# A quadrant swap of an 8192 x 8192 array: the right halves move to GpSimd's queue in eight-row copies

## The chip, the core and the metric

The kernel runs on one core of one Trainium2 chip. A core has five engines with an instruction queue each (TensorE, VectorE, ScalarE, GpSimd and SyncE) and 16 DMA engines that move data. The metric is the device time of one execution in microseconds. Three executions of the kernel before took 814.30, 814.51 and 814.64 us; their median is 814.51 us.

## The reference

```python
x = np.random.randn(8192, 8192).astype(np.float32)

def reference(x):
    return np.fft.ifftshift(x)
```

For even sizes this shifts both axes by half: `out[r, c] = x[(r + 4096) % 8192, (c + 4096) % 8192]`. Nothing is computed. The four quadrants of 64 MB each change places across the diagonal, so 268.44 MB are read and 268.44 MB are written.

## The kernel before

Input and output both lie in device memory, with 8192 float32 values, or 32 KB, to a row. The kernel uses no on-chip buffer: every transfer goes from the input straight to the output. Half a row is 16 KB, and since the column shift is exactly half a row, the left half of an output row is the right half of one input row, and the other way round.

The helper `copy` (line 26) takes a queue, a first output row, a first output column (0 for a left half, `hc` = 4096 for a right half) and an access pattern. It works out where the source begins (line 28) and issues one DMA on that queue (line 29). The pattern `back` (line 34) has three dimensions: 16 neighbouring rows, then 16 steps backwards by 16 rows each, then the 16 KB of a half row. So one copy moves the halves of 256 rows, 4 MB, and it is written as 16 shares of 16 rows each: share e takes the rows that lie e above the base row, then e - 16, e - 32 and so on down.

The outer loop (line 36) walks the output from the bottom to the top in stretches of 1024 rows, which are four blocks of 256. The inner loop (line 37) takes the four blocks in the order 3, 2, 1, 0. For each it issues the left half of block n on SyncE's queue (line 38) and the right half of block (n + 2) % 4 on ScalarE's queue (line 39). That makes 32 copies on each queue. No copy depends on another. The framework counts the landing of copies on semaphores, of which these copies use eight in turn, and a queue waits before it issues a copy until the earlier copy on the same semaphore has landed.

In the profile's lines the letter q after an engine's name (SPq, ACTq, POOLq) means the engine's instruction queue. q1 and q10 are the DMA queues on which the packets of the two issuing engines run. A packet is one half row of 16 KB, or a few bytes that count a landing.

Of the kernel before, what the change touches and what calls it, by code (L numbers as in the profile page):

```python
# [1 line left out]

# [4 lines left out]


ENGINES = 16


@with_exitstack
def kernel(
    ctx: ExitStack,
    tc: tile.TileContext,
    x: bass.AP,
    out: bass.AP,
):
    nc = tc.nc
    R, C = x.shape  # L20
    hr = R // 2
    hc = C // 2
    per = 16
    rows = ENGINES * per

    def copy(queue, row, col, dims):

        src = (row + hr) % R * C + (col + hc) % C
        queue.dma_start(
            out=bass.AP(out.tensor, out.offset + row * C + col, dims),  # L30
            in_=bass.AP(x.tensor, x.offset + src, dims),
        )

    back = [[C, ENGINES], [-ENGINES * C, per], [1, hc]]

    for first in range(R - 4 * rows, -1, -4 * rows):
        for n in (3, 2, 1, 0):
            copy(nc.sync, first + n * rows + rows - ENGINES, 0, back)
            copy(nc.scalar, first + (n + 2) % 4 * rows + rows - ENGINES, hc, back)


# [1 line left out]
_INS = ['x']  # L43
_OUTS = [((8192, 8192), 'float32')]


def kernel(**inputs):
    import numpy as _np
    import concourse.bacc as _bacc
    import concourse.tile as _tile  # L50
    from concourse import mybir as _mybir
    from concourse.bass_utils import run_bass_kernel_spmd as _run

    nc = _bacc.Bacc("TRN2", target_bir_lowering=False, num_devices=1)  # L54
    arrays, args = {}, []
    for name in _INS:
        a = _np.ascontiguousarray(inputs[name])
        if a.dtype.kind in "iu":
            a = a.astype(_np.int64)
        arrays[f"in_{name}_dram"] = a  # L60
        args.append(nc.dram_tensor(f"in_{name}_dram", a.shape, _mybir.dt.from_np(a.dtype), kind="ExternalInput").ap())
    for i, (shape, dtype) in enumerate(_OUTS):
        dt = _mybir.dt.from_np(_np.dtype(dtype))
        args.append(nc.dram_tensor(f"out_{i}_dram", shape, dt, kind="ExternalOutput").ap())
    with _tile.TileContext(nc) as tc:
        kernel(tc, *args)
    r = _run(nc, [arrays], core_ids=[0])
    got = tuple(r.results[0][f"out_{i}_dram"] for i in range(len(_OUTS)))
    return got[0]
```

## Time and profile before

| What | Value |
|---|---|
| median of three executions | 814.51 us |
| the profiled execution | 813.9 us |
| its span, first to last instruction | 812.1 us |
| bytes read, bytes written | 268.44 MB, 268.44 MB |
| mean rate of the copies | 331 GB/s |
| memory traffic over the span, both directions | 661 GB/s |
| DMA packets | 17408, of which 16384 are half rows |
| copies issued by SyncE, by ScalarE | 32, 32 |
| one issue on SyncE, on ScalarE (median) | 571 ns, 578 ns |
| issue to landing of one copy (median) | 101.0 us |

The span leaves out 1.8 us of the profiled execution's 813.9 us, which lie before the first and after the last instruction. The profiled execution lies 0.6 us under the median. The page's DMA row gives the mean busy share of the 16 DMA engines in 40 equal slices of the span, in tenths, and the row under it what they moved in each slice in GB/s. A copied byte counts once there, though it is both read and written. Busy shares are worked out from packet records, so over a short stretch they can come out above 1.

### The profile page before, as it was taken

How to read it: one execution, taken by the hardware profiler on the slowest of the kernel's cores; microseconds unless marked ns; L12 is line 12 of the kernel's file. 1: busy time of each engine (PE TensorE's matmuls, PEld its weight loads, DVE VectorE, ACT ScalarE, POOL GpSimd, SP SyncE). 2: the span in 40 equal slices, each digit the busy share in tenths (PEclk: the TensorE clock that was granted, in tenths of full speed). 3: DMA queues.
4: the chain of work that ended last, by engine and by line, in shares of the span. 5: the costliest groups of instructions: out<-in, count | busy, mean ns of one | idle time of the engine just before them, and what ended most of it. 6: DMA issues, size and time to landing. Idle time of an engine off the chain costs nothing. (4 is left out here: it accounts for less than half of the span.)

```text
span 812.1 us, 109 instructions
## 1 busy us (share of the span) xinstructions
POOL 0.2 (0%) x4
## 2 busy tenths in 40 slices
POOL 0000000000000000000000000000000000000000
DMA  9999999999999999999999999999999999999998
GB/s 306 332 329 337 333 332 335 328 324 337 329 336 337 332 334 334 334 336 331 332 329 330 337 328 334 339 331 333 332 320 333 330 331 330 336 332 337 334 333 286
DMA packets 17408, 268.44 MB, mean 331 GB/s; under 512 B 1024, under 2 KB 1024, under 8 KB 1024
## 3 DMA queue, kind: packets, MB, share of 16 engines
q1 hardware_dynamic: 8704, 134.22, 49.9%
q10 hardware_dynamic: 8704, 134.22, 49.1%
HBM read 268.44 MB, written 268.44 MB: 661 GB/s over the span
## 5 line engine op out<-in xcount | busy, mean ns | idle before, releaser
L54 POOL MEMSET const-bfloat16-1.0<- 128x1 bf16 x1 | 0.1, 102 | 0.0
L54 POOL MEMSET const-uint8-127<- 128x1 uint8 x1 | 0.1, 102 | 0.0
L54 POOL MEMSET const-float32-1.0<- 128x1 f32 x1 | 0.1, 99 | 0.0
L54 POOL MEMSET const-float32-0.0<- 128x1 f32 x1 | 0.1, 98 | 0.2 <-issue 0.2
## 6 DMA issues: line engine op xcount, KB each, us to landing
out_dram<-in_x_dram ACTq DMA_DIRECT2D x32, 4096.0 KB, 101.0
out_dram<-in_x_dram SPq DMA_DIRECT2D x32, 4096.0 KB, 101.0
```

The source lines that it names most:

```text
L54: nc = _bacc.Bacc("TRN2", target_bir_lowering=False, num_devices=1)
```

## The change

```diff
-    back = [[C, ENGINES], [-ENGINES * C, per], [1, hc]]
+    half = ENGINES // 2
     for first in range(R - 4 * rows, -1, -4 * rows):
         for n in (3, 2, 1, 0):
-            copy(nc.sync, first + n * rows + rows - ENGINES, 0, back)
-            copy(nc.scalar, first + (n + 2) % 4 * rows + rows - ENGINES, hc, back)
+            copy(nc.sync, first + n * rows + rows - ENGINES, 0, [[C, ENGINES], [-ENGINES * C, per], [1, hc]])
+            right = first + (n + 2) % 4 * rows + rows - half
+            for part in (0, half):
+                copy(nc.gpsimd, right - part, hc, [[C, half], [-ENGINES * C, per], [1, hc]])
```

The left halves are copied by the same 32 copies of 4 MB, on the same queue, in the same order. The right halves leave ScalarE's queue for GpSimd's. Each copy of 256 right halves becomes two of 128. The outermost dimension of their pattern has 8 rows in place of 16, and the steps stay at 16 rows. Part 0 takes the upper eight rows (the higher row numbers) of every 16 and part 8 the lower eight. That makes 64 copies of 2 MB, written as eight shares each; by the description of the change they go to the two groups of eight DMA engines in turn. The order of the blocks is the same. ScalarE then issues nothing.

## The prediction

> **What bounds the kernel now.** I read the page first: no engine computes, so the DMA rows carry everything. These are its lines of the span, the DMA slices, the queues and the memory traffic.
>
> ```profile
> span 812.1 us, 109 instructions
> DMA  9999999999999999999999999999999999999998
> GB/s 306 332 329 337 333 332 335 328 324 337 329 336 337 332 334 334 334 336 331 332 329 330 337 328 334 339 331 333 332 320 333 330 331 330 336 332 337 334 333 286
> DMA packets 17408, 268.44 MB, mean 331 GB/s; under 512 B 1024, under 2 KB 1024, under 8 KB 1024
> q1 hardware_dynamic: 8704, 134.22, 49.9%
> q10 hardware_dynamic: 8704, 134.22, 49.1%
> HBM read 268.44 MB, written 268.44 MB: 661 GB/s over the span
> ```
>
> The reader is to see that the DMA engines are busy from end to end (9 tenths or more in 39 of 40 slices; the queues' shares sum to 99.0%), and that the two queues split this evenly. A half row of 16384 bytes thus takes 0.990 x 812.1 x 16 / 16384 = 0.785 us of one DMA engine. The trace's packet records say what that consists of: the shortest half row took 0.608 us (26.9 GB/s), a third of them at most 0.612 us, the median one 0.726 us. So an engine can go 29% faster than it does on average. What holds it back is shared by the 16; I read it as the memory at 661 GB/s, though no row names it.
>
> Next the stretches in time (length, busy engines, clock, DMA share, GB/s), for the ends:
>
> ```profile
> 1.00:2.00 1.00, 0.00 (x0) 1.00 0.00 0
> 2.00:3.00 1.00, 0.00 (x0) 1.00 0.87 262
> ...
> 806.00:808.00 2.00, 0.00 (x0) 1.00 1.04 369
> 808.00:809.00 1.00, 0.00 (x0) 1.00 0.75 197
> 809.00:810.00 1.00, 0.00 (x0) 1.00 0.31 131
> 810.00:811.00 1.00, 0.00 (x0) 1.00 0.04 16
> 811.00:812.10 1.10, 0.00 (x0) 1.00 0.00 0
> ```
>
> Some 2 us pass before the first bytes, about 2 us at the end are lost to engines that finish unevenly, and 1.1 us follow the last bytes. All the rest is rate. The 38 inner slices have a mean of 332.4 GB/s, a lower quartile of 330.25, and ends of 320 and 339.
>
> Last the issues (nanoseconds, minimum, median and maximum), and what SyncE's queue waits for (total us, times, longest):
>
> ```profile
> L29 ACTq DMA_DIRECT2D out_dram<-in_x_dram x32: 577/578/884, 0.7 to 713.4; - x32
> L29 SPq DMA_DIRECT2D out_dram<-in_x_dram x32: 571/571/666, 0.7 to 709.0; - x32
> DMA to landing us min/median/max: 25.4/101.0/103.2
> SPq L29 <- DMA out_dram<-in_x_dram: 689.7, 28, 25.2
> ```
>
> SyncE issues for 32 x 0.571 = 18 us in all and waits 690 us for earlier copies: after its first four copies, each of the other 28 waits. The landing time agrees with eight copies in flight: 8 x 4.194 MB at 332 GB/s take 101 us. Issue is far from the bound; there is always a queue of work ahead of each DMA engine.
>
> **The change part by part.** The sum starts at the profiled execution's 813.9 us, 0.6 under the median; I add 0.6 at the end.
>
> *ScalarE's 32 issues go.* They took 32 x 0.578 = 18.5 us on an engine that does nothing else. Hidden; gain 0.
>
> *GpSimd gets 64 issues.* No row shows an issue on GpSimd. The nearest rows are POOL's memset at 0.10 us and ScalarE's longest issue at 0.884 us: 64 of them are 6 to 57 us, spread over 800. One 2 MB copy is needed every 12.6 us (2.097 MB at half of 332 GB/s), so the copies in flight hide them: cost 0. Without that cover it would be up to 57 us. Only the first issue can be seen. If GpSimd's first bytes come 0 to 1 us after SyncE's, the DMA engines already have left halves, and half of the delay returns at the end when right halves run alone: 0 to 0.5, I take 0.3.
>
> *More landing counts.* A copy of before counts with 16 small packets (1024 for 64). After, there are 96 copies: 512 packets for the left and 64 x 8 or 64 x 16 for the right, so 0 to 512 more. One takes 9 ns in the packet records: 512 x 9 / 16 engines = 0.3 us at most. I take 0.3.
>
> *SyncE's waits.* If SyncE has the eight semaphores alone, it waits for the copy eight before, not four, and 33.6 MB of left halves are in flight. Behind the waiting issue only further left copies are queued, and 8 copies of cover stand ahead. Cost 0. The same holds for GpSimd if it may keep several copies in flight: behind its waiting issue are only further right copies, and ScalarE waits for nobody. With less than one copy for each group, the cover is gone (last rival).
>
> *A packet of GpSimd's queue against one of ScalarE's.* No row shows it. The nearest is the difference of the two hardware queues, 49.9% against 49.1% for the same packets: 0.8% of 812.1 us, 6.5 us in time, or 13 ns for each of the 512 half rows that a queue has per engine. I take 0, since the engines wait for something shared, and keep -6.5 and +6.5 for the range.
>
> *Which rows are under way together.* In the diff this is the real change for the memory. Before, DMA engine e takes left and right halves of rows that are e modulo 16, in turn; 16 engines always stand on 16 different remainders. After, if the first group takes part 0, engine e has left halves of rows e but right halves of rows e + 8 modulo 16. When one engine has a left half and the engine eight further a right half, both stand on rows whose distance is a multiple of 16, or of 512 KB; this can happen about half of the time. The bounds are the slices: all at the best, 339 GB/s, is -1.9% or -16 us; all at the worst, 320, is +3.9% or +31 us. Nothing excludes either sign. The lower quartile is 0.65% under the mean, 5.2 us; I take half of it, since the meetings need opposite halves: +2.6. The row it is nearest to is the mean, as the bytes, packet sizes and number of streams per engine stay.
>
> The Trainium skill speaks against the change here. "DMA: Bandwidth & Descriptors", section "Latency and other measured facts", says that copies whose parallel streams lie a large power of two apart lose rate, 207 against 214 GB/s at a distance of 512 KiB and half at 4 MiB, and calls channel aliasing an inference. Carried over in full, 3.4% would make the sum about 842 us, an estimate. This trace shows no run with and without such meetings; its own slices bound the effect instead.
>
> *The end.* GpSimd's queue has drains of 34 to 66 ns now; with copies to wait for it may take as ScalarE's, up to 0.4 us. I take 0.3.
>
> Sum: 813.9 + 0.3 + 0.3 + 2.6 + 0.3 = 817.4, and 0.6 to the median: 818.0 us, 0.4% slower.
>
> **The rivals.** *A. Nothing of it matters.* All DMA engines stay busy at the same mean rate, and only the small terms remain: 815.4 us, within 0.2% (812.9 to 816.1), which is about what a measurement of this kernel can tell from no change. The even split and the flat slices speak for it; that the slices vary by several per cent says that the rate does depend on what meets what.
>
> *B. Faster.* The eight-row shift, with a stream whose phase is no longer tied to SyncE's, parts left and right traffic better than before. The place is the stall in each half row, 0.785 - 0.61 = 0.17 us. The price goes down to the best slice, 339 GB/s: 818 - 2.6 - 16 = 799 us. It decides as soon as the mean slice is above 333.4 GB/s (0.31% over 332.4, which takes the 815.4 us of rival A to 812.9). For it: a third of the packets already run unhindered, so the rest is a matter of meeting. Against it: memory traffic may have no more to give than 339.
>
> *C. A right packet costs more.* Every ns that a half row of GpSimd's queue holds an engine longer is 0.51 us of time. From 20 ns on it outweighs all else; at 60 ns, a twelfth of a median packet, it is +31. Together 828 to 849 us. For: a kind of queue that no row shows. Against: an engine that waits on shared memory can lose some ns for nothing.
>
> *D. The groups don't take turns,* or only one right copy is in flight. If all right halves fell on eight engines, those would move 134.22 + 67.11 = 201.3 MB at no more than 8 x 26.9 = 215 GB/s: at least 936 us. One copy in flight: an active group gives half of its time to right halves, so right gets a quarter of the rate, 44.7 MB by the time left is done; the other 89.5 MB at 215 instead of 332 GB/s add 147 us, 961. On whether they take turns, the same page, section "Why a DMA increments its semaphore by 16 and not by 1", says that a GpSimd copy whose outer dimension is 8 takes eight consecutive engines from a round-robin cursor. No row here shows it.
>
> **How the numbers follow.** The forecast (816.2 to 824, a small loss of rate) gets 0.38, A 0.13, B 0.35, C 0.11, D 0.03. Time 818.0. Faster comes from B, 0.35; same from A, 0.13; slower from the forecast, C and D, 0.52. B's end of 799 with a packet gain of some us beyond it makes the low end 796; the high end is 846, which leaves out the top of C, all of D and a little of B, less than 0.2. The likeliest case's own range is 816.2 to 824.
>
> **What would show it.** After: a DMA row of 9s; two queues of 134.22 MB each; the right one with 8192 half rows and 512 or 1024 small packets; shares still near 50% and 49%; inner slices with a mean near 331. SyncE's copies should land after about 8 x 4.194 MB / 166 GB/s = 202 us. The forecast is wrong in its main term if the mean inner slice is above 332.4; A is right if it is 332 to 333. C shows as a longer share of the right queue with the left one unchanged; D as a half-empty DMA row, or as one queue that ends long before the other. A GpSimd issue above 12 us would overturn the hiding of issues.

## The result, and the profile after

The changed kernel takes 817.21 us (median of 20 runs, 815.60 to 818.62), the kernel before 814.17 us (median of 20, 810.02 to 817.91). The ratio is 1.0037, with a 95% interval of 1.0026 to 1.0048. The forecast was 818.0 us and 0.4% slower.

The page of the changed kernel: the span, the GpSimd and DMA slices, the packets, the two queues and the memory traffic.

```profile
span 815.4 us, 145 instructions
POOL 2000000000000000000000000000000101011000
DMA  9999999999999999999999999999999999999998
GB/s 299 334 330 327 331 326 332 330 333 332 328 334 334 328 329 331 330 334 332 333 326 334 326 331 332 331 331 331 330 327 335 334 334 337 332 330 336 333 339 277
DMA packets 26113, 268.48 MB, mean 329 GB/s; under 512 B 9728, under 2 KB 9728, under 8 KB 9728
q0 software_dynamic: 17408, 134.25, 51.1%
q1 hardware_dynamic: 8704, 134.22, 48.2%
HBM read 268.44 MB, written 268.44 MB: 658 GB/s over the span
```

The DMA engines are as busy as before, and the span is 3.3 us longer at a slightly lower rate. Two things are new. GpSimd's queue (q0) has 17408 packets, not 8704: beside its 8192 half rows it carries 9216 packets of a few bytes. And the rate has two parts. Slices 2 to 29 have a mean of 330.7 GB/s (332.7 before); slices 31 to 39 have 334.4 (332.9 before). 28 slices of 20.4 us at 0.6% less are 3.4 us lost, nine at 0.45% more are 0.8 us won back; the rest of the 3.3 us lies at the ends. This is one execution of each kernel, and executions of the kernel before lie up to 1.0% apart, so the experiments below have to carry it.

What divides the two parts is seen in the packet split of two stretches. Here are the queue lines for 5 to 595 us, and then for 610 to 800 us.

```profile
q1 hardware_dynamic: 8427, 130.01, 64.5%
q0 software_dynamic: 8426, 65.06, 35.4%
...
q0 software_dynamic: 8235, 63.26, 100.1%
q1 hardware_dynamic: 15, 0.11, 0.2%
```

For some 600 us the left halves move at twice the rate of the right ones (130.01 MB against 65.06), with equally many packets of all sizes on both queues. By the packet records, the last left half ends at 611.8 us. After that right halves run alone, and the two kinds can no longer meet.

The issues (nanoseconds, minimum, median, maximum), the landing times, and what SyncE's and GpSimd's instructions wait for:

```profile
L29 POOL DMA_DIRECT2D out_dram<-in_x_dram x64: 589/589/738, 1.3 to 764.7; - x64
L29 SPq DMA_DIRECT2D out_dram<-in_x_dram x32: 593/15491/46425, 0.7 to 492.7; - x32
...
out_dram<-in_x_dram SPq DMA_DIRECT2D x32, 4096.0 KB, 117.8
out_dram<-in_x_dram POOLq DMA_DIRECT2D x64, 2048.0 KB, 91.6
...
SPq L69 <- DMA out_dram<-in_x_dram: 302.4, 1, 302.4
...
POOL out_dram L29 <- DMA out_dram<-in_x_dram: 712.8, 46, 25.8
```

GpSimd issues a copy in 0.589 us and waits 713 us for copies to land: issue is hidden. SyncE's issues now take a median of 15.5 us each, where they took 0.571; the first five take 0.6 to 0.8 us each, the sixth takes 15.4. It has nothing else to do, and at the end it waits 302 us for its last copies (line 69).

### The profile page after: what moved, and what is told of

It is laid out like the page before. It is cut to its first block, busy times and chain, and to the rows that moved or that the text cites. A ratio compares the mean times of both kernels' runs of the same rounds, so it can differ in the third digit from the quotient of the medians.

```text
span 815.4 us, 145 instructions
## 1 busy us (share of the span) xinstructions
POOL 38.0 (5%) x68
## 3 DMA queue, kind: packets, MB, share of 16 engines
q0 software_dynamic: 17408, 134.25, 51.1%
q1 hardware_dynamic: 8704, 134.22, 48.2%
## 4 chain that ended last, share of the span: by engine, by line
another core or an unknown queue 77%; DMA 11%; POOL 3%; issue 2%; POOLq 0%; PEldq 0%
DMA out_dram<-in_x_dram 11%; POOL out_dram L29 3%; POOLq L69 0%; PEldq L69 0%
## 5 line engine op out<-in xcount | busy, mean ns | idle before, releaser
L29 POOL DMA_DIRECT2D out_dram<-in_x_dram x64 | 37.8, 592 | 727.0 <-DMA out_dram<-in_x_dram 712.8
## 6 DMA issues: line engine op xcount, KB each, us to landing
out_dram<-in_x_dram SPq DMA_DIRECT2D x32, 4096.0 KB, 117.8
```

What stands on the lines that cost most here:

```text
L29: queue.dma_start(out=bass.AP(out.tensor, out.offset + row * C + col, dims), in_=bass.AP(x.tensor, x.offset + src, dims),)
```

## The experiments

Three theories were set against each other. *Rows*: after the change, an engine's right halves lie eight rows off its left halves, so left and right halves that are a multiple of 512 KB apart are under way together. *Small packets*: the extra packets on GpSimd's queue cost time. *Drift*: the two streams no longer keep their distance. Each ratio is against the kernel before on the same chip in the same hour; the chips differ (the kernel before took 812.6 to 822.7 us on them), so times are compared only within a chip.

**GpSimd's queue alone.** The kernel before, with one word changed.

```diff
-            copy(nc.scalar, first + (n + 2) % 4 * rows + rows - ENGINES, hc, back)
+            copy(nc.gpsimd, first + (n + 2) % 4 * rows + rows - ENGINES, hc, back)
```

> Right halves on GpSimd as 32 copies of 4 MB over 16 rows, so the queue changes and nothing else. Three theories for the 3 us that the change costs (817.2 against 814.2). Small packets: the 9216 packets of a few bytes on GpSimd's queue (144 per copy, where 16 would count the landing) cost 9 ns each and take turns from right halves. Rows: left and right halves on rows a multiple of 512 KB apart meet. Drift: left halves run at twice the rate of right ones for 604 us, so the two streams no longer keep their distance of 512 rows. Small packets expects 512 small packets on the GpSimd queue, equal rates of left and right, and 814.2 +- 0.8 us. Rows expects 814.2 (every engine stays on its own row remainder). Drift expects 814.2 if the rates are equal. If all are wrong and GpSimd's queue itself costs, 817.

Measured: 813.98 us against 812.62, ratio 1.0018 (0.9995 to 1.0041), which does not settle a small cost. Its two queue lines settle where the small packets come from:

```profile
q0 software_dynamic: 8704, 134.22, 50.0%
q1 hardware_dynamic: 8704, 134.22, 49.1%
```

512 small packets for 32 copies are 16 a copy, and both kinds of half rows keep step to the end. The extra packets belong to the eight-row copies, not to the queue.

**The two parts in the other order.** The changed kernel, in which only the order of the eight-row parts is swapped.

```diff
-            for part in (0, half):
+            for part in (half, 0):
```

> The changed kernel with the two eight-row parts issued in the other order, so that (if the first part goes to the first group) each DMA engine has left and right halves of the same row remainder, as before the change. Small packets and drift expect what the changed kernel takes, 817.2 +- 0.8 us, with left halves again at twice the rate. Rows expects the loss to go: 814.2 to 814.8 us.

Measured: 812.86 us against 812.62, ratio 1.0002 (0.9985 to 1.0019). The loss is gone, while 9216 small packets and the two-to-one split are still there. Since the changed kernel had not run on this chip, both orders were then run on one chip.

> The changed kernel unaltered, beside the kernel before and the swapped order on one chip. Its ratio to the kernel before was 1.0037. All theories of what in it is slow expect 1.003 to 1.004 again; that it was a difference of chips or of the hour expects 1.000 +- 0.001, as for the swapped order.

> The swapped order of the two eight-row parts again, on the same chip as the changed kernel. Rows expects 1.000 +- 0.001 of the kernel before and 2.5 to 3 us less than the changed kernel. Small packets and drift, which the swap leaves as they are, expect the changed kernel's time within 1 us.

Measured: the changed kernel 829.21 us (828.16 to 830.50), ratio 1.0085 (1.0066 to 1.0104); the swapped order 822.98 us (821.67 to 825.24), ratio 1.0010 (0.9996 to 1.0025); the kernel before 822.07. The order of two issues is worth 6.2 us here, and the ranges do not overlap. That is more than twice the 2.5 to 3 us that rows expected, and the changed kernel's ratio is more than twice the expected 1.003 to 1.004; why this chip makes more of it is open. The rates in 40 slices, first of the changed kernel on this chip, then of the swapped order:

```profile
GB/s 297 327 321 326 327 322 328 326 322 327 328 328 328 319 332 325 328 323 328 328 323 327 329 322 322 326 323 328 324 326 328 331 333 335 326 331 329 328 334 281
```

```profile
GB/s 296 326 329 330 327 331 331 331 330 330 328 326 331 328 331 328 332 328 330 331 328 331 330 332 329 327 331 333 332 329 315 328 329 329 334 329 331 325 331 260
```

Slices 2 to 29 have a mean of 325.6 against 329.7: this is where the time goes, in the part in which left and right halves are mixed. In slices 31 to 39, with right halves alone, it is 330.6 against 327.9, so nothing is lost there. By the packet records it is the right halves that lose it: between 5 and 490 us one takes a mean of 840 ns in the changed kernel and 801 ns in the swapped order (a left half 779 and 787), and between 630 and 790 us, alone, 784 and 785.

Small packets and drift are the same in both and cannot make this difference. Rows, as stated, can. What this shows is that the time depends on which right rows run beside which left rows. That the loss comes from two engines a multiple of 512 KB apart is the picture that rows gives of it; no row shows which engine moved what, so the picture itself is argued.

**More small packets.** Copies of four rows, issued so that each engine keeps its row remainder.

```diff
-    half = ENGINES // 2
+    half = ENGINES // 4
...
-            for part in (0, half):
+            for part in (12, 8, 4, 0):
```

> Right halves on GpSimd as 128 copies of 1 MB over 4 rows, issued so that each engine keeps its row remainder if the groups of four come in turn. Small packets expects 128 x (12 x 16 + 16) = 26624 of them on GpSimd's queue, left halves at four times the rate of right ones at first, and 26112 x 9 ns / 16 = 14.7 us more than 814.2 if each costs its 9 ns: 829 us; a third of that, 819, if most of it is hidden as it is in the changed kernel's second phase. Rows expects 814 to 815. Drift expects about 817, as the left stream runs ahead too, if for a shorter time.

```profile
DMA packets 43521, 268.55 MB, mean 329 GB/s; under 512 B 27136, under 2 KB 27136, under 8 KB 27136
q0 software_dynamic: 34816, 134.32, 50.7%
```

The number is as expected: 34816 - 8192 = 26624 = 128 x (12 x 16 + 16). So a GpSimd copy over k engines carries 16 packets that count it and, as the counts suggest, for each of the 16 - k engines it does not use as many tiny packets as the others have half rows. The packet records also show left halves at four times the rate of right ones, until the last left half ends at 509 us. That fits engines that take a packet from each queue in turn, whatever its size. The price is far less than the 14.7 us of 9 ns each: 815.0 against 812.62 us, ratio 1.0037 (1.0018 to 1.0055), so 1.5 to 4.5 us for the whole version, its 26112 more small packets included. In the swapped eight-row kernel a third as many cost nothing that shows. Rows failed here: it expected 814 to 815 us where the kernel before takes 814.2, a ratio of 1.001 at most. Drift's 817, a ratio of 1.0034, came nearest, but the swapped order drifts as well and loses nothing that shows. What costs the 1.5 to 4.5 us, the small packets, the drift or groups of four that do not fall as assumed, is open.

**The row theory at its strongest.** The kernel before, with each share made of 16 neighbouring rows, so that the 16 engines of a copy stand 512 KB apart.

```diff
-    back = [[C, ENGINES], [-ENGINES * C, per], [1, hc]]
+    back = [[ENGINES * C, ENGINES], [-C, per], [1, hc]]
...
-            copy(nc.sync, first + n * rows + rows - ENGINES, 0, back)
-            copy(nc.scalar, first + (n + 2) % 4 * rows + rows - ENGINES, hc, back)
+            copy(nc.sync, first + n * rows + ENGINES - 1, 0, back)
+            copy(nc.scalar, first + (n + 2) % 4 * rows + ENGINES - 1, hc, back)
```

> The kernel before with share e as 16 neighbouring rows, so that the 16 DMA engines of a copy stand 16 rows, 512 KB, apart and all on the same row remainder as long as they keep step. This is the largest dose of what the row theory blames. Rows expects a loss of 2% or more (830 us up); if the row remainder has nothing to do with the rate, 814 +- 1 us.

Measured: 855.30 us against 822.07, ratio 1.0401 (1.0378 to 1.0423). The slices and the memory traffic:

```profile
GB/s 292 313 314 314 313 315 322 310 320 314 318 315 310 324 313 312 318 318 316 314 315 308 317 318 322 308 327 311 314 315 311 321 311 316 319 314 318 314 308 293
HBM read 268.44 MB, written 268.44 MB: 628 GB/s over the span
```

The rate lies under that of the swapped order on the same chip in every inner slice, and packet sizes, queues and counts are those of the kernel before. So which addresses are moved at one time changes the rate, here without GpSimd. Two distances changed together: the engines of one copy stand 512 KB apart in place of 32 KB, and the successive half rows of one engine 32 KB apart in place of 512 KB. No run separates the two. The Trainium skill's page "DMA: Bandwidth & Descriptors", section "Latency and other measured facts", gives 207 against 214 GB/s for a distance of 512 KiB, 3.4%; 4.0% was measured here.

**The shift on the two queues of before.** This was to show the row effect without GpSimd. Right copies were shifted by eight rows; the rows that stick out at the ends of each half of the array went in four small copies of 1 KB pieces on ScalarE's queue, 0.52 MB in all.

```diff
+            block = first + (n + 2) % 4 * rows
+            if (block + rows) % hr:
+                copy(nc.scalar, block + 8 + rows - ENGINES, hc, back)
+            else:
+                copy(nc.scalar, block + 8 + rows - 2 * ENGINES, hc, [[C, ENGINES], [-ENGINES * C, per - 1], [1, hc]])
+                for edge in (block + rows - 8, block + rows - hr):
+                    copy(nc.scalar, edge, hc, [[hc // 16, 16], [C, 8], [1, hc // 16]])
```

> The kernel before, both queues as before, with the right copies' rows shifted by eight (the eight rows that stick out at the ends of each half of the array go in four small copies of 1 KB pieces, 1 MB in all, estimated at under 1 us in all). Each DMA engine then has left halves of rows e and right halves of rows e + 8 modulo 16, for the whole execution, with no GpSimd, no extra small packets on a software queue and equal rates. Rows expects 1.003 to 1.006 of the kernel before. Anything tied to GpSimd's queue expects 1.000 to 1.001.

Measured: 830.92 us against 822.07, ratio 1.0094 (1.0059 to 1.0128), a loss as rows expected, though larger than its 1.003 to 1.006. But the control, shifted by 16 rows so that every engine keeps its remainder (8 replaced by 16, and the edge rows to match), lost more, on a third chip with the shift by eight beside it:

> The control for the shift by eight rows: the same kernel with the right copies shifted by 16 rows, with as many small edge copies in 1 KB pieces, but every DMA engine on one row remainder for left and right as in the kernel before. Rows expects the inner slices of the kernel before and at most 1.004 of its time, all of it from the edge copies and the end. If the edge copies and not the rows made the loss of the shift by eight (1.0094), this takes 1.009 too.

> The shift by eight rows again, on the same chip as its control. Rows expects 4 to 8 us more than the control; the edge copies alone expect no difference.

Measured: the control 828.18 us (823.52 to 834.65), ratio 1.0181 (1.0137 to 1.0225); the shift by eight 820.77 us, ratio 1.0083 (1.0056 to 1.0111); the kernel before 813.86. Rows failed here: it expected the shift by eight to take 4 to 8 us more than the control, and it took 7.4 us less. Both runs have a cost that rows does not name, so they can't be counted for it, and until that cost is explained they stand against it. The slices of the control, and below them those of the shift by eight on the same chip, show part of the cost:

```profile
GB/s 302 339 332 328 330 335 332 326 333 329 330 328 327 330 329 332 323 327 332 327 323 330 328 329 334 325 326 328 329 327 326 334 327 330 327 333 335 323 327 204
```

```profile
GB/s 290 334 318 336 329 329 327 329 329 331 332 332 330 335 330 330 332 326 330 334 331 334 329 324 331 338 330 334 330 333 330 334 329 331 331 330 334 331 330 249
```

The edge pieces are 32 packets for each engine, and each takes a turn from right halves: left halves end 26 us before right ones in the control (797.9 against 823.8 us by the packet records; 32 x 0.79 us is 25), and the last slice, 204 GB/s, shows engines that finish unevenly. Against the 286 of the kernel before in its profile, (286 - 204) x 20.6 us / 330 is some 5 us of the control's 14.3. The inner slices are low as well, with a mean of 329.2 against 330.7 for the shift by eight and 333.1 for all copies on SyncE's queue on this chip (below). Why is open.

The last run made the shift by eight without these pieces: the edge rows go in two GpSimd copies at the start, two half rows for each engine. This is the edit against the shift by eight.

```diff
+    for row in (hr - 8, 0):
+        nc.gpsimd.dma_start(
+            out=bass.AP(out.tensor, out.offset + row * C + hc, [[C, 8], [hr * C, 2], [1, hc]]),
+            in_=bass.AP(x.tensor, x.offset + (row + hr) * C, [[C, 8], [-hr * C, 2], [1, hc]]),
+        )
...
-                for edge in (block + rows - 8, block + rows - hr):
-                    copy(nc.scalar, edge, hc, [[hc // 16, 16], [C, 8], [1, hc // 16]])
```

> The shift by eight rows without the 1 KB pieces that spoilt its first form (they made the left halves run ahead, and the control with a shift of 16 lost as much). The 32 rows that stick out go in two GpSimd copies of 8 x 2 half rows at the start, two half rows for each DMA engine; everything else is on the two queues of the kernel before, in step. Rows expects a loss in the inner slices and a ratio of 1.004 to 1.009, since left and right halves a multiple of 512 KB apart can meet for the whole execution. If the loss of the shifted kernels came from the pieces and the broken step alone, and the loss of the changed kernel from something that only GpSimd's two groups bring, 1.000 +- 0.0015.

Measured: 825.44 us (822.04 to 832.31) against 822.74, ratio 1.0050 (1.0024 to 1.0076). Its queues:

```profile
q10 hardware_dynamic: 8672, 133.70, 50.4%
q1 hardware_dynamic: 8704, 134.22, 48.7%
q0 software_dynamic: 96, 0.52, 0.2%
```

The two streams keep step, GpSimd moves 0.52 of 268 MB, and the loss is inside the range that rows gave. It has no control with a shift of 16 in this clean form, so what small cost the uneven cut into copies has by itself is not separated. A version that was to show rows with no edge pieces at all, with share e of a right copy on row remainder 15 - e and both queues as before, gave no time.

**One queue for everything.** The kernel before with both copies on SyncE's queue, or both on GpSimd's.

```diff
-            copy(nc.scalar, first + (n + 2) % 4 * rows + rows - ENGINES, hc, back)
+            copy(nc.sync, first + (n + 2) % 4 * rows + rows - ENGINES, hc, back)
```

> All 64 copies of the kernel before on SyncE's queue, left and right in the same order as before in turn. Each DMA engine then has one queue and keeps to one row remainder. Rows expects what the kernel before takes within 0.3%, as no two engines meet. If the rate after the left halves are done in the changed kernel (334 GB/s against 330 to 331) comes from having one queue rather than from the end of the meetings, this is 0.3 to 0.5% faster than the kernel before.

> All 64 copies of the kernel before on GpSimd's queue, 16 rows and 4 MB each. If GpSimd's queue costs anything per half row, this shows it twice as clearly as the half-and-half kernel, whose ratio of 1.0018 (0.9995 to 1.0041) leaves it open: 1.003 to 1.004. If it costs nothing: 1.000 +- 0.001.

Measured against 813.86 us: SyncE alone 815.05 us, ratio 1.0035 (1.0002 to 1.0069); GpSimd alone (both lines) 816.01, ratio 1.0026 (1.0004 to 1.0049). One queue is not faster, so the higher rate of the changed kernel's second part is not the merit of having one queue. And GpSimd's queue costs no more than SyncE's that shows: the two ratios differ by 0.0009, less than either interval is wide. Why one queue for everything, of either kind, loses some 0.3% is open. None of the versions beats the kernel before.

## Why the prediction was right, point by point

- *What bounds it.* Right: the shared rate behind busy DMA engines. Another distance between the same packets moved the time by 4%, while doubled issues and 8704 more packets moved it little.
- *Which rows are under way together: +2.6 us.* The right term, the right sign, and it carries the result. The changed kernel loses 3.0 us by the medians in the result. On the one chip that had both orders, the swap takes 6.2 us of the 7.1 us loss away; on another the swapped order alone is at 1.0002. Its size came from half of a quartile of the slices, a way of choosing between wide bounds and no calculation of the meetings; that it fell so near in the result is partly luck, since another chip more than doubles it. The picture behind it, engines a multiple of 512 KB apart, has the swap and the shares of neighbouring rows for it, and against it, until they are explained, the four-row copies and the shift by 16 rows. That the first part goes to the first group of engines was an assumption. No row shows which DMA engine carried what; the effect of the swap is what the assumption foretells.
- *Landing counts: +0.3.* No cost shows, and the count was wrong. The bound of 1024 on GpSimd's queue missed the packets for unused engines: 9216 came. At 9 ns each the excess would be 4.6 us, but the swapped order, which has all of them, is at 1.0002 and 1.0010, and the intervals end at 1.5 and 2.1 us.
- *The even split and the landing times.* Wrong. Over the whole span the shares are 51.1% and 48.2%, but up to 595 us they are 35.4% for right and 64.5% for left halves. SyncE's copies were to land after 202 us and landed after 117.8. Two steps failed. The working took equal turns to mean equal bytes, and left halves ran at twice the rate. It also took eight copies in flight: 117.8 us at 130.01 MB in 590 us, 220 GB/s, are 26 MB or six copies, an estimate, and the sixth issue is the first that takes long. SyncE does not wait for an earlier copy before an issue at all; it is held inside it. None of this cost time that shows, as the engines stay busy whoever is ahead.
- *Issues hidden: 0.* Right. 64 x 0.59 = 38 us on GpSimd, inside the 6 to 57 of the bounds, beside 713 us of waiting. The first half row on GpSimd's queue starts 3.6 us after SyncE's by the packet records, not 0 to 1; but ScalarE's started 2.9 us after before the change, so 0.7 us are new. What the 0.3 us for it were worth was not measured.
- *A packet of GpSimd's queue: 0, within 6.5 us either way.* Right as far as the runs tell: 1.0018 (0.9995 to 1.0041) for half of the traffic, and no difference to SyncE for all of it.
- *The end: +0.3.* By the packet records the last bytes land 1.8 us before the span's end, against 1.2 before: +0.6.
- *The rivals.* Rival A is outside the interval. B's picture, that the shift moves the meetings, was right with the other sign: the changed mean of 331.5 GB/s is below 332.4. C's sign, a longer share of the right queue, is there (51.1% against 49.1%), but the left share fell as well, and GpSimd's queue alone is no slower than SyncE's alone. One queue does end long before the other, a sign of D, but the DMA row stays at 9: left halves had simply gone at twice the rate.

## What to carry to other kernels

When DMA engines are busy throughout and yet slower than their fastest packets, look at which addresses they move at the same time; the order of two issues can decide it without changing a byte or a count. A harmless-looking split of a copy changes three things at once (which engine has which rows, how many turns each queue gets, how many tiny packets there are), so undo them one by one. A control needs the same side effects as the thing that it controls; here the version with small edge copies and no shift by eight lost more than the effect under test, and part of that loss is unexplained.

## What the runs showed of the hardware that was not expected

- A GpSimd copy over 8 engines put 128 extra tiny packets on its queue beside 16 counts, one over 4 engines 192; copies over 16 engines put none.
- The DMA engines took packets from two queues in turn, by number and not by bytes: the tiny packets gave the left halves two thirds of the rate (four fifths with copies over 4 engines), without an effect on the total that shows for the first; the second took 1.5 to 4.5 us more, from them or from something else.
- Where SyncE did not wait for earlier copies before an issue, the issue took a median of 15.5 us in place of 0.571 (11.8 us with all copies on its queue), from the sixth copy of 4 MB on. What holds it there was not tried.
